# Differential attention in a decoder trunk: the scores of a head as one stretch of row halves in six PSUM banks, the rest of the head in a fixed order behind it

## The chip, the cores and the metric

The kernel runs on one core of one Trainium2 chip. The metric is the device time of one execution, in microseconds (us). Before the change three runs took 1916.96 us in the median (1916.87 to 1918.63).

## The reference

The program is a decoder trunk of two layers over 512 tokens of width 1024, in float32. Each layer is FFN, token mixer, cross-attention, FFN, each closed by a layer norm. The mixer of the first layer is causal differential attention with 8 heads; only this mixer is touched:

```python
def diff_attention(x, w_qkv, w_o, lam_q, lam_k, subln_g, cos, sin, lam_init):
    q, k, v = jnp.split(x @ w_qkv, 3, axis=-1)
    q = rope(q.reshape(B, S, H, 2, dk), c5, s5)      # H = 8, dk = 64: two maps per head
    k = rope(k.reshape(B, S, H, 2, dk), c5, s5)
    v = v.reshape(B, S, H, 2 * dk)
    ...
    def block(args):                                  # blocks of 128 queries
        qblk, i = args
        s = jnp.einsum('bqhcd,bkhcd->bhcqk', qblk, k).astype(jnp.float32) * scale
        s = jnp.where(mask, s, jnp.finfo(jnp.float32).min)
        p = jax.nn.softmax(s, axis=-1)
        a = p[:, :, 0] - lam * p[:, :, 1]
        return jnp.einsum('bhqk,bkhe->bqhe', a.astype(v.dtype), v)
    o = lax.map(block, (qb, jnp.arange(nb)))
    ...
    o = o * lax.rsqrt(jnp.mean(jnp.square(o), axis=-1, keepdims=True) + LN_EPS)
    o = o * subln_g.astype(jnp.float32) * (1.0 - lam_init)
    return o.reshape(B, S, H * 2 * dk).astype(x.dtype) @ w_o
```

## The kernel before

Every float32 operand is split into a high and a low part of a rounded format, and every product is three matmuls (high by high, high by low, low by high; lines L210 to L212 in the projections). Tokens stand in four blocks of 128. A head has 128 rows of q and of k: rows 0 to 63 are its first map, rows 64 to 127 its second.

The mixer is woven from two generators. `da_main` does the projections: v of two heads, then q and k of each head, and after the last of them the output projection of heads 0 to 3. `da_side` does the attention of a head once its q and k are there. `weave` runs the main one, counts its estimated time, and takes one unit of the side whenever enough has passed: `GAP` (900 ns) times the weight that the last unit yielded. The framework's scheduler then fixes one order for each engine, in which high-priority instructions are put early. On the chip each engine works through its own order and waits at its head.

For block i of a head (queries of block i against keys 0 to (i+1)x128) the side does:

- `da_scores`: the scores of both maps on TensorE (PE). For i = 0 and 1 both maps come from one matmul per term into one PSUM bank (L1154), by keys that `da_key` has copied apart into tiles `low` with zeros in the other map's rows (`keys_apart`; four copies per head on ScalarE, L1139). For i = 2 and 3 each map has its own bank, and the matmul uses only its 64 rows of the array (L1159). Then, for each map, one VectorE instruction adds the mask, negates, writes the result to `p` in SBUF and takes the row minimum (L1164, with a read of the accumulator), and ScalarE takes the exponential with its row sum (L1167).
- `da_mix`: on VectorE, the reciprocal of the second map's sum, the coefficient, and p0 + coefficient x p1 (L1176, L1177, L1178).
- `da_turn`: the i+1 blocks of p are transposed on PE (L496, tile `pt`), and split into the pair `a` by ScalarE and VectorE (L125, L126).
- `da_out`: the product with v on PE (L1199, L1200, tile `po`). After blocks 1 and 3 ScalarE copies (L1205), VectorE adds (L1206), ScalarE squares with a sum (L1209). After block 3 GpSimd works out the norm's factor f (L1216 to L1219).
- `da_scale`: o times f on ScalarE (L1228; for the last head half on VectorE); `da_turn_out`: o is transposed on PE (L496) and split.

The side works by steps over all blocks of all heads: in step s it does the scores of block s, the mix of block s-1, the turn of block s-2, the output of block s-3, the scale of a head five steps behind its last block, and the turn of its output six behind.

The banks for `sc`, `pt` and `po` come from three PSUM pools in turn (px, py, yz, two buffers each: six banks); the projections have two further banks.

Of the kernel before, what the change touches and what calls it, by code (L numbers as in the profile page):

```python
# [17 lines left out]
P = 128  # L18
D = 1024
S = 512  # L20
NT = S // P
# [7 lines left out]
DA_H = 8  # L29
# [4 lines left out]
NEG = -float(2.0**100)  # L34
# [1 line left out]


V_FIRST, LEAD, GAP = 6, 6000, 900
W_SC, W_T, W_O, W_E = (1.1, 1.4, 1.8, 2.2), (0.5, 0.7, 0.9, 1.1), (0.4, 0.8, 0.6, 1.1), (0.6, 0.8)
LM, LT, LO, LS = 1, 2, 3, 5  # L40
HALVES = (slice(0, DA_DK), slice(DA_DK, P))

FFN_TURNS = (((0, 1, 2), ()), ((3, 4), (0, 1)), ((5, 6), (2, 3)), ((7, 8), (4, 5)), ((9, 10), (6, 7)))
# [53 lines left out]
WAIT = object()  # L97


def drain(units):  # L100
    for _ in units:
        pass
# [7 lines left out]
class Trunk:  # L110
# [80 lines left out]
    def mm(self, name):  # L191
        return self.mmp.tile([P, S], F32, tag="mm", name=name)
# [937 lines left out]

    def da_key(self, ps):


        k, t = self.pair("qk"), self.da_rope(ps)
        apart = self.keys_apart[len(self.heads) % 2]
        self.split(k[0], k[1], t)
        for whole, part in zip(k, apart):
            for m, rows in enumerate(HALVES):
                self.nc.scalar.copy(part[rows, m], whole[rows, : 2 * P].bitcast(F32))  # L1139
        return k, apart  # L1140

    def da_scores(self, st, i):

        nc = self.nc
        q, k, n = st["q"], st["k"], (i + 1) * P
        qi, kn = slice(i * P, n), slice(0, n)
        mx, rc, cf = self.small("mx"), self.small("rc", (P, 1)), self.small("cf", (P, 1))
        sm = st["sm"][:, i]
        mm, terms = nc.tensor.matmul, ((0, 0), (1, 0), (0, 1))
        if i < 2:  # L1150
            both = self.aux("sc")[:, : 2 * n].rearrange("p (m n) -> p m n", m=2)
            sc = [both[:, m] for m in range(2)]
            for a, b in terms:
                mm(both, q[a][:, qi], k[1][b][:, :, kn], start=a == b, stop=b == 1)  # L1154
        else:
            sc = [self.aux("sc")[:, :n] for m in range(2)]
            for a, b in terms:
                for m, rows in enumerate(HALVES):
                    mm(sc[m], q[a][rows, qi], k[0][b][rows, kn], start=a == b, stop=b == 1)  # L1159
        p = [self.tmp("p")[:, :n] for m in range(2)]  # L1160
        with self.tc.high_priority():
            for m in range(2):
                least = mx[:, m : m + 1]
                nc.vector.tensor_tensor_reduce(  # L1164
                    p[m], sc[m], self.mask[:, S - n :], -1.0, -NEG, ALU.add, ALU.min, least
                )
                nc.scalar.activation(  # L1167
                    p[m], p[m], AF.Exp, bias=least, scale=-1.0, accum_out=sm[:, m : m + 1]
                )
        st["m", i] = p, sm, rc, cf  # L1170

    def da_mix(self, st, i):

# [89 lines left out]

    def da_side(self):

        n = DA_H * NT
        for s in range(n + LS + 2):
            h, i = divmod(s, NT)
            if s < n:
                while h >= len(self.heads) or self.clock < self.heads[h][0] + LEAD:  # L1270
                    yield WAIT
                self.da_scores(self.heads[h][1], i)
                yield W_SC[i]
            h, i = divmod(s - LM, NT)
            if 0 <= s - LM < n:
                self.da_mix(self.heads[h][1], i)
            h, i = divmod(s - LT, NT)
            if 0 <= s - LT < n:
                self.da_turn(self.heads[h][1], i)
                yield W_T[i]  # L1280
            h, i = divmod(s - LO, NT)
            if 0 <= s - LO < n:
                while len(self.heads[h][1]["v"]) < NT:
                    yield WAIT
                self.da_out(self.heads[h][1], i)
                yield W_O[i]
            h, i = divmod(s - LS, NT)
            if 0 <= s - LS < n and i == NT - 1:
                self.da_scale(self.heads[h][1])
                yield W_E[0]  # L1290
            h, i = divmod(s - LS - 1, NT)
            if 0 <= s - LS - 1 < n and i == NT - 1:
                self.oT[h] = self.da_turn_out(self.heads[h][1])
                yield W_E[1]

    def diff_attention(self, layer, ln):
        self.keys_apart = [self.pair("low", (P, 2, 2 * P)) for i in range(2)]
        for pair in self.keys_apart:
            for t in pair:
                for m, rows in enumerate(HALVES):  # L1300
                    self.nc.gpsimd.memset(t[rows, 1 - m].bitcast(F32), 0.0)
# [459 lines left out]
```

## Time and profile before

| what | before |
| --- | --- |
| median of three runs | 1916.96 us |
| the profiled execution | 1915.99 us, its span 1914.2 us |
| PE busy | 1898.0 us (99%) |
| VectorE (DVE) busy | 1551.7 us (81%) |
| ScalarE (ACT) busy | 1016.6 us (53%) |
| GpSimd (POOL) busy | 319.3 us (17%) |
| granted TensorE clock, mean | 0.999 |

The span runs from the first to the last instruction of one profiled execution. PE counts matmuls, PEld the weight loads that overlap them. A row of the timeline has the start in us, the duration in us, engine, line, operation, output and inputs, shapes and count; in square brackets the idle time before it and what ended it. Matmuls are pipelined: a row's duration is longer than the distance to the next one's start, and it is the distance that counts. The same holds for VectorE and ScalarE. The attention lies between 340 and 560 us.

### The profile page before, as it was taken

The page shows a single profiled execution, that of the slowest core. Times are in us where ns is not written, and L with a number is a line of the kernel's source. Part 1 is how long each engine was busy: PE and PEld are TensorE (multiplying, and loading weights), DVE is VectorE, ACT ScalarE, POOL GpSimd, SP SyncE. Part 2 cuts the span into 40 slices and gives each one's busy share as a digit, 9 for nine tenths or more (in the row PEclk, how much of TensorE's full clock was granted, in tenths as well). Part 3 has the DMA queues.
Part 4 walks back from the last instruction along what each step waited for, and adds up shares of the span by engine and source line. Part 5 has one row for each costly group of instructions (what it writes and reads, how often), then busy time and mean ns, then how long its engine had stood idle before and what let it go on. Part 6 is the DMA issues. An engine that isn't in the chain of part 4 may idle for free.

```text
span 1914.2 us, 32507 instructions
## 1 busy us (share of the span) xinstructions
PE 1898.0 (99%) x13088; PEld 1732.0 (90%) x13088; DVE 1551.7 (81%) x2250; ACT 1016.6 (53%) x1578; POOL 319.3 (17%) x282
## 2 busy tenths in 40 slices
PE   9999999999999999999999999999999999999998
PEld 8999998888879888999998999999898889999996
DVE  7888889888867558889888988898787568998886
ACT  6555454566745435655553655555455436555552
POOL 3112121111110002221220311212130012211210
PEclk9999999999999999999999999999999999999999
DMA  9978772332225317987785687878344438867861
GB/s 249 215 176 177 177 139 78 91 89 67 89 67 161 116 60 194 193 175 164 143 191 171 117 180 166 181 164 186 101 132 133 137 84 174 178 156 168 189 130 54
DMA packets 246743, 277.96 MB, mean 145 GB/s; under 512 B 8256, under 2 KB 212544, under 8 KB 246592
## 3 DMA queue, kind: packets, MB, share of 16 engines
q0 software_dynamic: 92928, 92.29, 31.5%
q1 hardware_dynamic: 153664, 183.59, 29.9%
q8 instruction: 103, 1.69, 0.4%
q14 instruction: 48, 0.39, 0.1%
HBM read 273.75 MB, written 2.10 MB: 144 GB/s over the span
## 4 chain that ended last, share of the span: by engine, by line
PE 82%; DVE 11%; ACT 3%; DMA 2%; issue 1%; POOL 1%; SPq 0%; DVEq 0%; ACTq 0%; POOLq 0%
PE x L210 7%; PE x L211 7%; PE x L212 7%; PE z L210 4%; PE z L211 4%; PE z L212 4%; PE ps L210 4%; PE ps L212 4%; PE ps L211 4%; PE px L212 2%; PE px L210 2%; PE px L211 2%; PE y L212 2%; PE y L210 2%; PE y L211 2%; PE pz L212 1%
## 5 line engine op out<-in xcount | busy, mean ns | idle before, releaser
L715 POOL DMA_DIRECT2D ra<-in_ffn_w_in_dram x132 | 170.8, 1316 | 981.8 <-DVE wl L722 966.2
L720 ACT CAST wh<-ra 128x1024 fp32r<-128x1024 f32 x176 | 185.1, 1054 | 206.9 <-PE x L211 65.7
L722 DVE TENSOR_TENSOR wl<-ra,wh 128x1024 fp32r<-128x1024 f32 x176 | 214.2, 1222 | 66.5 <-ACT wh L720 66.1
L210 PE MATMUL x<-xe,wh 128*128 128x256 f32 x704 | 194.8, 277 | 0.0
L211 PE MATMUL x<-xe,wh 128*128 128x256 f32 x704 | 194.6, 276 | 0.0
L212 PE MATMUL x<-xe,wl 128*128 128x256 f32 x704 | 194.5, 276 | 0.0
L720 ACT CAST wh<-rc 128x1024 fp32r<-128x1024 f32 x132 | 138.9, 1053 | 101.6 <-PE x L211 41.4
L125 ACT CAST wh<-b 128x1024 fp32r<-128x1024 f32 x112 | 117.8, 1051 | 130.5 <-PE x L211 67.2
L722 DVE TENSOR_TENSOR wl<-rc,wh 128x1024 fp32r<-128x1024 f32 x132 | 160.0, 1220 | 24.9 <-ACT wh L720 24.9
L126 DVE TENSOR_TENSOR wl<-b,wh 128x1024 fp32r<-128x1024 f32 x112 | 136.8, 1221 | 40.2 <-ACT wh L125 40.2
L210 PE MATMUL x<-xh,wh 128*128 128x256 f32 x536 | 148.5, 277 | 0.0
L211 PE MATMUL x<-xl,wh 128*128 128x256 f32 x536 | 148.2, 276 | 0.0
L212 PE MATMUL x<-xh,wl 128*128 128x256 f32 x536 | 148.2, 276 | 0.0
L211 PEld LDWEIGHTS x<-xe,wh 128*128 128x128 f32 x704 | 132.3, 188 | 1.4
L210 PEld LDWEIGHTS x<-xe,wh 128*128 128x128 f32 x704 | 132.1, 188 | 1.3
L212 PEld LDWEIGHTS x<-xe,wl 128*128 128x128 f32 x704 | 132.2, 188 | 0.0
L126 DVE TENSOR_TENSOR wl<-raw,wh 128x1024 fp32r<-128x1024 f32 x64 | 82.2, 1288 | 42.0 <-ACT wh L125 41.2
L211 PEld LDWEIGHTS x<-xl,wh 128*128 128x128 f32 x536 | 100.7, 188 | 0.7
L210 PEld LDWEIGHTS x<-xh,wh 128*128 128x128 f32 x536 | 100.6, 188 | 0.7
L212 PEld LDWEIGHTS x<-xh,wl 128*128 128x128 f32 x536 | 100.6, 188 | 0.0
L125 ACT CAST wh<-raw 128x1024 fp32r<-128x1024 f32 x64 | 66.4, 1048 | 60.6 <-PE xq L211 20.2
L210 PE MATMUL z<-xe,wh 128*128 128x256 f32 x352 | 97.4, 277 | 0.0
(451 smaller groups left out, 6289.7 us busy)
## 6 DMA issues: line engine op xcount, KB each, us to landing
ra<-in_ffn_w_in_dram POOLq DMA_DIRECT2D x132, 512.0 KB, 6.9
rc<-in_ffn_w_in_dram SPq DMA_DIRECT2D x88, 512.0 KB, 5.9
b<-in_ffn_w_out_dram SPq DMA_DIRECT2D x76, 512.0 KB, 4.8
ra<-in_ffn_w_in_dram SPq DMA_DIRECT2D x44, 512.0 KB, 5.0
rc<-in_ffn_w_in_dram POOLq DMA_DIRECT2D x44, 512.0 KB, 7.5
raw<-in_xa_wkv_dram SPq DMA_DIRECT2D x16, 1024.0 KB, 5.4
raw<-in_da_w_qkv_dram SPq DMA_DIRECT2D x16, 512.0 KB, 5.2
raw<-in_xa_wq_dram SPq DMA_DIRECT2D x8, 1024.0 KB, 5.2
```

The costliest lines, as they stand in the source:

```text
L125: self.nc.scalar.copy(hi, src),
L126: self.nc.vector.tensor_sub(lo, src, hi.bitcast(F32)),
L210: self.first_mm = mm(out, w[0], x[0], start=start, stop=False, skip_group_check=again)
L211: mm(out, w[0], x[1], start=False, stop=False, skip_group_check=again)
L212: self.last_mm = mm(out, w[1], x[0], start=False, stop=stop, skip_group_check=again)
L715: nc.gpsimd.dma_start(t, source(*block), accum_op=ALU.add)
L720: hi = nc.scalar.copy(v[0], raw)
L722: lo = nc.vector.tensor_sub(v[1], raw, v[0].bitcast(F32))
```

## The change

The copies apart (`keys_apart`, their zeroing on GpSimd and the four ScalarE copies per head) go. `da_scores` now does a whole head: all matmuls of its four blocks stand in one stretch, each on the 64 rows of its map, 24 of them (4 blocks x 3 terms x 2 maps), in the block order 1, 0, 2, 3. They take six banks at once: two for block 1, two that blocks 2 and 0 share, two for block 3. Behind it come the mask, minimum and exponential of all blocks in the same order. `da_side` goes head by head: scores, the turn of the previous head's output, then the fixed list `STEPS`, then the scale. The pool `p` has 8 buffers instead of 6.

```diff
-W_SC, W_T, W_O, W_E = (1.1, 1.4, 1.8, 2.2), (0.5, 0.7, 0.9, 1.1), (0.4, 0.8, 0.6, 1.1), (0.6, 0.8)
-LM, LT, LO, LS = 1, 2, 3, 5
+W = dict(scores=2.0, turn=(1.0, 1.0, 1.2, 1.5), out=(0.6, 0.8, 1.2, 2.0), scale=0.8, last=0.8)
+STEPS = (
+    ("mix", 1), ("mix", 0), ("mix", 2), ("turn", 0), ("mix", 3), ("turn", 1),
+    ("out", 0), ("turn", 2), ("out", 1), ("turn", 3), ("out", 2), ("out", 3),
+)
+SC_ORDER = (1, 0, 2, 3)
...
     def da_key(self, ps):
-        k, t = self.pair("qk"), self.da_rope(ps)
-        apart = self.keys_apart[len(self.heads) % 2]
-        self.split(k[0], k[1], t)
-        for whole, part in zip(k, apart):
-            for m, rows in enumerate(HALVES):
-                self.nc.scalar.copy(part[rows, m], whole[rows, : 2 * P].bitcast(F32))
-        return k, apart
+        k = self.pair("qk")
+        self.split(k[0], k[1], self.da_rope(ps))
+        return k
...
+    def da_scores(self, st):
+        one, two, three = ([self.aux("sc") for m in range(2)] for i in range(3))
+        banks = {
+            0: [t[:, 3 * P :] for t in two],
+            1: [t[:, : 2 * P] for t in one],
+            2: [t[:, : 3 * P] for t in two],
+            3: three,
+        }
+        for i in SC_ORDER:
+            qi, kn = slice(i * P, (i + 1) * P), slice(0, (i + 1) * P)
             for a, b in terms:
                 for m, rows in enumerate(HALVES):
+                    mm(banks[i][m], q[a][rows, qi], k[b][rows, kn], start=a == b, stop=b == 1)
+        for i in SC_ORDER:
...
     def da_side(self):
+        for h in range(DA_H):
+            while h >= len(self.heads) or self.clock < self.heads[h][0] + LEAD:
+                yield WAIT
+            st = self.heads[h][1]
+            self.da_scores(st)
+            yield W["scores"]
+            if h:
+                self.oT[h - 1] = self.da_turn_out(self.heads[h - 1][1])
+                yield W["last"]
+            for step, i in STEPS:
+                if step == "out":
+                    while len(st["v"]) < NT:
+                        yield WAIT
+                getattr(self, "da_" + step)(st, i)
+                if step != "mix":
+                    yield W[step][i]
+            self.da_scale(st)
+            yield W["scale"]
...
-            bufs = dict(low=4, rt=2, a=4, p=6, o=2, qk=8, _x=0, v=4, oT=11, mask=1)
+            bufs = dict(low=4, rt=2, a=4, p=8, o=2, qk=8, _x=0, v=4, oT=11, mask=1)
```

Lines of the changed program stand ten or fewer behind those of the old one (L1162 is the score matmul, L1171 the mask and minimum, L1174 the exponential, L1183 to L1185 the mix, L1235 the scale, L1212 the copy of o, L1216 the squares). How it moves instructions is shown at three places of head 1; rows are the engine's order, with line, operation, output and inputs, shape, and a count where equal ones follow each other.

PE at the scores of head 1 (`v` and `q` are projections). Before, one block's scores between two steps of the projection of v:

```order
L212 MATMUL v<-wh,xl 128x256
L1154 MATMUL sc<-low,qk 128x512 x3
L210 MATMUL v<-wh,xh 128x256
L211 MATMUL v<-wl,xh 128x256
L212 MATMUL v<-wh,xl 128x256
```

Now:

```order
L222 MATMUL v<-wh,xl 128x256
L1162 MATMUL sc<-qk 128x256 x6
L1162 MATMUL sc<-qk 128x128 x6
L1162 MATMUL sc<-qk 128x384 x6
L1162 MATMUL sc<-qk 128x512 x6
L220 MATMUL v<-wh,xh 128x256
```

All four blocks now stand together. Behind them PE has 18 matmuls of v, four transposes of the previous head's o, 6 matmuls of v, and then the transpose of p of block 0, which needs the mix of block 0.

VectorE at the mix of block 0 of head 1 (`p` tiles are numbered; `mx` rows read the minimum; `rc` and `cf` are reciprocal and coefficient). Before, that mix follows its own block's minimum:

```order
L1164 ISA p_4332,mx_4325<-sc_4328,mask_3828 128x128
L1164 ISA mx_4325 128x1
L1164 ISA p_4333,mx_4325<-sc_4328,mask_3828 128x128
L1164 ISA mx_4325 128x1
L1176 RECIPROCAL rc_4326<-sd_4205 128x1
L1177 SCALAR_TENSOR_TENSOR cf_4327<-sd_4205,nlam_4033,rc_4326 128x1
L1178 SCALAR_TENSOR_TENSOR p_4332<-p_4333,cf_4327,p_4332 128x128
```

Now (p_4415 is block 0; the rows of 128x384 and 128x512 are blocks 2 and 3):

```order
L1171 ISA p_4425,mx_4421<-sc_4376,mask_3816 128x384
L1171 ISA mx_4421 128x1
L1171 ISA p_4433,mx_4430<-sc_4377,mask_3816 128x512
L1171 ISA mx_4430 128x1
L1171 ISA p_4434,mx_4430<-sc_4378,mask_3816 128x512
L1171 ISA mx_4430 128x1
L1183 RECIPROCAL rc_4413<-sd_4235 128x1
L1183 RECIPROCAL rc_4422<-sd_4235 128x1
L1184 SCALAR_TENSOR_TENSOR cf_4414<-sd_4235,nlam_4021,rc_4413 128x1
L1184 SCALAR_TENSOR_TENSOR cf_4423<-sd_4235,nlam_4021,rc_4422 128x1
L1185 SCALAR_TENSOR_TENSOR p_4415<-p_4416,cf_4414,p_4415 128x128
```

The mix of block 0 now stands behind the minima of all four blocks; in heads 1, 3, 5, 6 and 7 the reciprocal, coefficient and mix of block 1 stand between the minima of block 1 and those of block 0.

ScalarE at the exponentials of head 1. Before, the scale of head 0 has one block's exponentials behind it:

```order
L1209 ACTIVATE po,sq<-o 128x128
L1228 ACTIVATE o<-o,f 128x128 x3
L1167 ACTIVATE p,sd<-p,mx 128x512 x2
L125 CAST a<-pt 128x256
L130 ACTIVATE qk<-rt 128x512
```

Now:

```order
L1212 COPY o<-po 128x256
L135 CAST v<-v 128x4x128
L1216 ACTIVATE po,sq<-o 128x128 x2
L1235 ACTIVATE o<-o,f 128x128 x4
L1174 ACTIVATE p,sd<-p,mx 128x256 x2
L1174 ACTIVATE p,sd<-p,mx 128x128 x2
L1174 ACTIVATE p,sd<-p,mx 128x384 x2
L1174 ACTIVATE p,sd<-p,mx 128x512 x2
```

All exponentials of head 1 stand behind the four scales of head 0, and those behind the last squares of head 0; so it is in heads 3, 5, 6 and 7 too, while in heads 2 and 4 the scales stand far ahead.

More of the change, by code (lines that the diff above doesn't have):

```diff
@@ L38 @@
 V_FIRST, LEAD, GAP = 6, 6000, 900
-W_SC, W_T, W_O, W_E = (1.1, 1.4, 1.8, 2.2), (0.5, 0.7, 0.9, 1.1), (0.4, 0.8, 0.6, 1.1), (0.6, 0.8)
-LM, LT, LO, LS = 1, 2, 3, 5
+W = dict(
+    scores=2.0,
+    turn=(1.0, 1.0, 1.2, 1.5),
+    out=(0.6, 0.8, 1.2, 2.0),
+    scale=0.8,
+    last=0.8,
+)
+STEPS = (
+    ("mix", 1), ("mix", 0), ("mix", 2), ("turn", 0), ("mix", 3), ("turn", 1),
+    ("out", 0), ("turn", 2), ("out", 1), ("turn", 3), ("out", 2), ("out", 3),
+)
+SC_ORDER = (1, 0, 2, 3)
 HALVES = (slice(0, DA_DK), slice(DA_DK, P))
@@ L1131, in da_key @@
     def da_key(self, ps):
-        k, t = self.pair("qk"), self.da_rope(ps)
-        apart = self.keys_apart[len(self.heads) % 2]
-        self.split(k[0], k[1], t)
-        for whole, part in zip(k, apart):
-            for m, rows in enumerate(HALVES):
-                self.nc.scalar.copy(part[rows, m], whole[rows, : 2 * P].bitcast(F32))
-        return k, apart
-    def da_scores(self, st, i):
-        nc = self.nc
[L1145 to L1156, printed above, removed]
+        k = self.pair("qk")
@@ new lines, in da_key @@
+        self.split(k[0], k[1], self.da_rope(ps))
+        return k
+    def da_scores(self, st):
+        nc = self.nc
+        q, k, mm, terms = st["q"], st["k"], self.nc.tensor.matmul, ((0, 0), (1, 0), (0, 1))
+        one, two, three = ([self.aux("sc") for m in range(2)] for i in range(3))
[7 more added lines that the diff above has]
+            qi, kn = slice(i * P, (i + 1) * P), slice(0, (i + 1) * P)
@@ L1157, in da_scores @@
             for a, b in terms:
                 for m, rows in enumerate(HALVES):
[L1159 to L1169, printed above, removed]
@@ L1170, in da_scores @@
-        st["m", i] = p, sm, rc, cf
+                    mm(banks[i][m], q[a][rows, qi], k[b][rows, kn], start=a == b, stop=b == 1)
+        for i in SC_ORDER:
+            n = (i + 1) * P
+            mx, rc, cf = self.small("mx"), self.small("rc", (P, 1)), self.small("cf", (P, 1))
+            sm = st["sm"][:, i]
+            p = [self.tmp("p")[:, :n] for m in range(2)]
+            with self.tc.high_priority():
+                for m in range(2):
+                    least = mx[:, m : m + 1]
+                    nc.vector.tensor_tensor_reduce(
+                        p[m], banks[i][m], self.mask[:, S - n :], -1.0, -NEG, ALU.add, ALU.min, least
+                    )
+                    nc.scalar.activation(
+                        p[m], p[m], AF.Exp, bias=least, scale=-1.0, accum_out=sm[:, m : m + 1]
+                    )
+            st["m", i] = p, sm, rc, cf
@@ L1264, in da_side @@
     def da_side(self):
[L1266 to L1294, printed above, removed]
@@ L1296, in diff_attention @@
-    def diff_attention(self, layer, ln):
[L1297 to L1301, printed above, removed]
+        for h in range(DA_H):
[16 more added lines that the diff above has]
+            yield W["scale"]
@@ L1302, in diff_attention @@
+        self.oT[h] = self.da_turn_out(st)
+        yield W["last"]
+    def diff_attention(self, layer, ln):
         self.mask = self.act("mask", (P, S), mybir.dt.bfloat16)
```

## Prediction

> **What bounds the kernel now.** I read the page first (busy shares, the chain that ended last), then the attention stage by windows, then the timelines of PE, VectorE and ScalarE in it.
>
> ```profile
> span 1914.2 us, 32507 instructions
> PE 82%; DVE 11%; ACT 3%; DMA 2%; issue 1%; POOL 1%; SPq 0%; DVEq 0%; ACTq 0%; POOLq 0%
> 340.00:560.00 220.00, 218.51 (x1300) 182.32 (x1299) 175.35 (x441) 137.46 (x373) 37.84 (x51) 1.00 0.28 85
> ```
>
> The last row is the stage: of 220 us PE is idle for 1.5, VectorE for 45, ScalarE for 83. PE sets the end here, so the change is worth what it takes from PE's own work, less every wait that it puts into PE's order.
>
> **What it takes from PE.** The distance between starts is the price of a matmul.
>
> ```profile
> 368.95 0.51 PE L1154 MATMUL sc<-low,qk 128*128 128x256 f32 x3
> 369.30 0.40 PE L210 MATMUL k<-xh,wh 128*128 128x512 f32 x1
> ...
> 370.00 0.85 PE L1154 MATMUL sc<-low,qk 128*128 128x512 f32 x3
> 370.69 0.40 PE L210 MATMUL k<-xh,wh 128*128 128x512 f32 x1
> ...
> 371.86 0.40 PE L212 MATMUL k<-xh,wl 128*128 128x512 f32 x1
> 372.19 0.79 PE L1159 MATMUL sc<-qk 64*128 64x384 f32 x6
> ...
> 373.25 0.40 PE L211 MATMUL k<-xl,wh 128*128 128x512 f32 x1
> ...
> 379.83 0.22 PE L1200 MATMUL po<-v,a 128*128 128x128 f32 x1
> 379.89 0.33 PE L210 MATMUL v<-wh,xh 128*128 128x256 f32 x1
> ```
>
> Three matmuls of 256 columns take 0.35 (369.30-368.95), of 512 columns 0.70, so 0.117 and 0.232 each; 128 columns take 0.06. The stretch of six row halves with 384 columns takes 373.25-371.86, less the two paces of 0.232 that stand there anyway: 0.93. Six matmuls one behind the other would take 6x0.174 (three quarters of 0.232) = 1.04, and more with any cost of switching; three pairs side by side take 0.52. So the halves run side by side, and entering and leaving the row-half mode costs 0.40. By that a stretch of six with 512 columns takes 3x0.232 + 0.40 = 1.10.
>
> A head before: 0.35 + 0.70 + 0.93 + 1.10 = 3.08. Now one stretch: 3x(0.06+0.117+0.174+0.232) + 0.40 = 2.15. That is 0.93 less per head, 7.4 for eight. The pairs with 128 columns are the one new form; if they only kept the pace of 256 columns, each head would lose 3x0.057, 1.4 in all. In head 7 the new order splits the last six matmuls by three of the output projection: one more switch, 0.40, and one pair taken apart, 0.23. **Gain 6.7 us.** The four copies per head off ScalarE and the zeroing off GpSimd are worth nothing here: neither engine is the bound.
>
> **What it puts into PE's order.** Before, the turn of a block came a whole step after its mix. Now the transpose of block 0 stands, in head 1, 24 matmuls of 256 columns and four transposes behind the scores.
>
> ```profile
> 389.90 0.60 PE L496 MATMUL pt<-ident,p 128*128 128x128 f32 x4
> 390.25 0.48 PE L210 MATMUL q<-xh,wh 128*128 128x512 f32 x1
> 390.57 0.39 PE L211 MATMUL q<-xl,wh 128*128 128x512 f32 x1
> ```
>
> Four transposes cost 0.67-0.23 = 0.44. Let T be the start of the first score pair; of the 0.40 for switching, 0.10 lies before it. PE is at that transpose at T + 1.75 + 0.30 + 24x0.117 + 0.44 = T+5.3. VectorE must by then have done, in the order shown, the minima of all four blocks and two mixes:
>
> ```profile
> 384.03 0.29 DVE L1164 CUSTOM_DVE_ANT_0 p<-sc,mask 128x128 f32<-128x128 f32 x1
> 384.25 0.08 DVE L1164 DVE_READ_ACCUMULATOR2_ANT mx<- 128x1 f32 x1
> ...
> 388.34 0.42 DVE L1164 CUSTOM_DVE_ANT_0 p<-sc,mask 128x256 f32<-128x256 f32 x1 [0.63 <-PE sc L1154]
> 388.69 0.08 DVE L1164 DVE_READ_ACCUMULATOR2_ANT mx<- 128x1 f32 x1
> ...
> 393.34 0.56 DVE L1164 CUSTOM_DVE_ANT_0 p<-sc,mask 128x384 f32<-128x384 f32 x1
> 393.82 0.08 DVE L1164 DVE_READ_ACCUMULATOR2_ANT mx<- 128x1 f32 x1
> ...
> 395.28 0.16 DVE L1176 RECIPROCAL rc<-sd 128x1 f32<-128x1 f32 x1 [0.90 <-ACT p L1167]
> 395.48 0.22 DVE L1177 SCALAR_TENSOR_TENSOR cf<-sd,nlam,rc 128x1 f32<-128x1 f32 x1
> 395.73 0.62 DVE L1178 SCALAR_TENSOR_TENSOR p<-p,cf 128x384 f32<-128x384 f32 x1
> ...
> 399.29 0.68 DVE L1164 CUSTOM_DVE_ANT_0 p<-sc,mask 128x512 f32<-128x512 f32 x1
> 399.90 0.08 DVE L1164 DVE_READ_ACCUMULATOR2_ANT mx<- 128x1 f32 x1
> ```
>
> One minimum of 128, 256, 384, 512 columns takes 0.22, 0.35, 0.48, 0.61; the next one starts with the read. Two maps of four blocks: 3.3. Reciprocal and coefficient take 0.2 and 0.25 when each waits for the one before. From the scores to the minimum:
>
> ```profile
> 387.44 0.86 PE L1154 MATMUL sc<-low,qk 128*128 128x512 f32 x3
> ```
>
> The third of these starts 0.46 on, at 387.90; the minimum starts at 388.34, 0.44 later, and with 256 columns 0.12 earlier. Block 1 is then ready at T + 0.10 + 2x0.117 + 0.32 = T+0.65.
>
> ScalarE comes between, since the mix of block 1 needs its exponentials and, in heads 1, 3, 5, 6 and 7, stands ahead of the other minima:
>
> ```profile
> 388.98 0.49 ACT L1167 ACTIVATE p<-p,mx 128x256 f32<-128x256 f32 x1
> ...
> 389.47 0.49 ACT L1167 ACTIVATE p<-p,mx 128x256 f32<-128x256 f32 x1
> ...
> 394.55 0.60 ACT L1167 ACTIVATE p<-p,mx 128x384 f32<-128x384 f32 x1
> ```
>
> One exponential of 256 columns takes 0.49; from the start of the second to the reciprocal is 395.28-394.55 = 0.73 for 384 columns, some 0.62 for 256.
>
> ```profile
> 427.59 0.41 DVE L1206 TENSOR_TENSOR o<-o,po 128x256 f32<-128x256 f32 x1
> ...
> 428.47 0.28 ACT L1209 ACTIVATE po<-o 128x128 f32<-128x128 f32 x1
> ...
> 430.31 0.99 ACT L1228 ACTIVATE o<-o,f 128x128 f32<-128x128 f32 x3 [1.44 <-POOL f L1219]
> 431.21 0.71 ACT L1167 ACTIVATE p<-p,mx 128x512 f32<-128x512 f32 x1
> ```
>
> These show ScalarE waiting for GpSimd's f (second square to scale 1.84) with an exponential behind three scales (0.30 each). Now all exponentials of heads 1, 3, 5, 6, 7 stand behind four. From the last output matmul: 0.6 for the copy (an estimate: 0.2 as from scores to minimum less the matmul's own pace, and 0.4 as of a pass of this width), add to scale 430.31-427.59 = 2.7, four scales 1.2: ScalarE is free 4.5 us behind it. PE has only 24 matmuls of 256 columns (2.8) and 0.1 there, so that is T+1.6, against T+1.1 when the minimum is ready.
>
> Head 1 by steps: exponentials of block 1 at T+1.6 and 2.1, reciprocal 2.7, coefficient 2.9, mix 3.2 to 3.55, then 2.6 of minima (0.43+0.96+1.22) to 6.2, two reciprocals and coefficients 0.7, mix of block 0 with its way to PE 0.4: T+7.3. **PE waits 2.0**, where it waited for nothing. Behind it the mixes of blocks 2 and 3 and a weight split stand before the low part of block 0, and output 0 waits 0.3 more. Head 3 has the same order: 2.3 each.
>
> Heads 2 and 4: no scales in the way, but the next head's q ended only 1.4 (six matmuls of 512 columns) before the scores, and its rotation stands first on VectorE:
>
> ```profile
> 398.07 0.74 DVE L1119 STREAM_SHUFFLE rt<-q 128x512 f32<-128x512 f32 x1
> ...
> 398.89 1.30 POOL L1121 TENSOR_TENSOR rt<-rt,ropeS 128x512 f32<-128x512 f32 x1 [17.63 <-DVE rt L1119]
> ...
> 400.51 0.69 DVE L1122 TENSOR_TENSOR rt<-rt 128x512 f32<-128x512 f32 x1
> ```
>
> Shuffle to GpSimd 0.8, GpSimd 1.3, the sum 0.65: with 0.2 ahead of it VectorE is free 2.95 after q's end, which is T+1.45, 0.8 late. Then 3.3 of minima, 0.6 and 0.6 for q's low part and a weight split, 0.8 for reciprocals and coefficients, two mixes 0.8: T+7.6 against T+5.3, 2.3 each. Head 0 has one split more and only 12 matmuls of 512 columns (2.8) between scores and transpose, but more time ahead: T+7.4 against T+4.9, 2.5.
>
> Head 5 has q's rotation ahead of the add, the squares and so of f: the scales end at T+2.9 instead of T+1.6, and it waits 1.3 more than head 1, 3.3. In head 6 they end at T+3.0, 1.4 more; k's rotation stands between the last minimum and the mix of block 0 and adds 2.4 (0.8 + 1.3 + 0.6 less what else runs in it, 0.3); PE comes 0.7 later: 2.0 + 1.4 + 2.4 - 0.7 = 5.1. Head 7 has the split stretch and more of the output projection ahead, PE at T+6.4 against T+7.3: 0.9. Sum: 2.5 + 2.3 + 2.3 + 2.3 + 2.3 + 3.3 + 5.1 + 0.9 = 21.0, **21 us**.
>
> Bounds of the waits: with VectorE free at T+0.65 and ScalarE at once, the chain ends at T+6.8, 1.5 in a typical head and 11 in all; if each head went like head 6, 41. I take 21, built from the orders themselves, nearer to the low end since nothing in the trace makes every head like head 6. Waits that PE has today in the stage (1.5) I leave as they are.
>
> [...]
>
> **Sum.** 1914.2 - 6.7 + 21 = 1928.5 of span; with the 1.8 between span and time (1915.99-1914.2), 1930.3. The profiled execution lies 1.0 under the median, so 1931.
>
> **Rivals.** (a) *The saving decides; faster.* PE's waits for the mix stay under 0.35 on average, so under 3 of the 6.7. For it: VectorE's 45 idle us in the stage. Against it: idle in the stage does not help a queue that must do four blocks of minima in order. About 1911. (b) *The short end.* VectorE and ScalarE are ready in time, VectorE finding the coefficient of block 1 early too, waits of 7 to 10: 1917 to 1920, no change by what can be told apart here (0.2%, 3.8 us). (c) *Banks.* The scores take all six banks, the sixth last held by the squares of the previous head, which end some 2 us after its last output; the sixth is wanted 4 after it. If the squares queue behind casts by 3 instead of 0, five heads wait 1 more each: 1936. (d) *The clock.* Waits of 3 to 5 us are new; in the whole stage PE idled 1.5.
>
> ```profile
> 1.25 3.17 PE L120 MATMUL idle<-hb 128*128 128x512 bf16 x7 [1.25 <-DVE hb L569]
> 4.21 2.01 PE L496 MATMUL pt<-ident,X 128*128 128x128 f32 x8
> ```
>
> After the idle start seven matmuls of 512 columns took 2.96, 0.42 each instead of 0.23. If each head's wait brings this back for as many, 8x7x0.19 = 11 us more: 1942. [...]
>
> **How the numbers follow.** Forecast 0.57, its own range 1923 to 1940; (a) 0.10; (b) 0.16; (c) 0.12; (d) 0.05. The range 1918 to 1941 leaves out (a), the lower edge of (b) and the far end of (d). Faster 0.10; same 0.16; slower 0.74.
>
> **What would show it.** Right: score pairs start together and a stretch costs 2.1 to 2.2; PE's waits list the transpose of p behind the mix of VectorE, eight times, 1 to 5 us, longest in head 6; ScalarE's exponentials start behind the scales. Wrong: those waits sum to less than 7; or PE waits before the scores rather than behind them (c); or the pairs do not overlap at 128 columns; or the granted clock falls in the stage (d).

## The result, and the profile after

| what | before | after |
| --- | --- | --- |
| median (runs) | 1917.09 us (1916.87 to 1918.63, 4) | 1940.37 us (1939.35 to 1943.91, 4) |
| the profiled execution | 1915.99 us, span 1914.2 us | 1939.43 us, span 1937.6 us |
| PE busy | 1898.0 us (99%) | 1901.4 us (98%) |
| granted TensorE clock, mean | 0.999 | 0.995 |

The ratio is 1.0124, 95% interval 1.0111 to 1.0136: 23.3 us slower, where 14 were forecast. The median lies inside the stated range (1918 to 1941) by only 0.6 us. First the page's own rows of the changed kernel (the span; the chain that ended last, by engine) and the window of the attention stage. Such a window row has the stretch, its length, the busy time of PE, PEld, VectorE, ScalarE and GpSimd, each with its number of instructions, then the granted clock, the DMA share and GB/s.

```profile
span 1937.6 us, 32560 instructions
PE 80%; DVE 12%; ACT 3%; DMA 2%; issue 2%; POOL 1%; SPq 0%; DVEq 0%; POOLq 0%; ACTq 0%
340.00:560.00 220.00, 200.17 (x1236) 170.25 (x1235) 163.91 (x418) 119.34 (x321) 36.57 (x49) 0.96 0.23 70
```

PE is still the engine that sets the end, but in these 220 us it is now idle for 20 instead of 1.5, it gets fewer instructions through (1236 against 1300), and its clock, 1.00 before, is 0.96. All of the difference lies in this stage: from 6 us before the first score matmul to the first matmul of the next stage (the memory's keys) before needed 216.2 us, after 239.3, and 23.1 is the growth of the whole span (23.4) but for 0.3.

I made an account of PE over that stretch by the distances between the starts of its matmuls. Each distance is its matmul's own pace (0.232 for 512 columns, 0.117 for 256 and so on), and what is over is put down to a half clock if it lies in such a window, to a wait if it is over 0.25, and to switching and small losses otherwise. The numbers are worked out, not rows of a view; records missing from a trace move something between the first two columns, so they are read together, and a column is good to some 0.5 us.

| us | stage | paces | switching, small losses | waits | half clock |
| --- | --- | --- | --- | --- | --- |
| before | 216.2 | 195.4 | 18.8 | 1.9 | 0 |
| after | 239.3 | 192.2 | 16.4 | 22.8 | 7.5 |

The work itself fell by 5.6 (214.2 to 208.6), waits rose by 20.9, and 7.5 came from the clock. The list of PE's waits in the changed kernel (weight loads, which meet the wait first: 20.0 at the transposes against 17.6 on the matmuls; total, times, longest) says where:

```profile
PEld pt L506 <- DVE p L1185: 20.0, 7, 5.0
PEld sc L1162 <- DVE mx L1171: 2.6, 1, 2.6
```

Seven waits are transposes of block 0 behind VectorE's mix, in heads 0 to 6. The eighth, in head 7, is inside the scores: its last three matmuls, which belong to block 3, wait until VectorE has done a minimum of block 2. VectorE comes to that minimum late, because it waits for ScalarE's exponentials of block 1 first:

```profile
552.51 0.16 DVE L1183 RECIPROCAL rc<-sd 128x1 f32<-128x1 f32 x1 [1.84 <-ACT p L1174]
```

```profile
554.40 0.96 PE L1162 MATMUL sc<-qk 64*128 64x512 f32 x3 [2.14 <-DVE mx L1171]
```

I take what matmul and minimum share to be a bank of PSUM; which bank ties these two was not traced. On PE's timeline head 1 looks like this:

```profile
388.19 0.28 PE L222 MATMUL v<-wh,xl 128*128 128x256 f32 x1
388.40 2.18 PE L1162 MATMUL sc<-qk 64*128 64x256 f32 x24
390.51 0.39 PE L220 MATMUL v<-wh,xh 128*128 128x256 f32 x1
390.74 0.28 PE L221 MATMUL v<-wl,xh 128*128 128x256 f32 x1
...
393.77 0.28 PE L222 MATMUL v<-wh,xl 128*128 128x256 f32 x1
395.47 0.33 PE L506 MATMUL pt<-ident,p 128*128 128x128 f32 x1 [1.42 <-DVE p L1185]
```

Measured as the prediction measured a stretch, up to the second matmul behind it, the score stretch takes 390.74 - 388.19 - 2x0.117 = 2.32, where 2.15 was worked out. So the saving is 0.76 a head and not 0.93. Most of the difference lies in the pairs of 128 columns: the two matmuls of a pair start within 0.004 of each other, but two of three pairs keep a distance of 0.11 to the next pair instead of 0.06. PE is at the transpose at T+5.5 (T = 388.40) and gets it at T+7.1. In between, ScalarE's first exponential and VectorE's end of the minima in the same head:

```profile
390.04 0.50 ACT L1174 ACTIVATE p<-p,mx 128x256 f32<-128x256 f32 x1
```

```profile
394.00 0.69 DVE L1171 CUSTOM_DVE_ANT_0 p<-sc,mask 128x512 f32<-128x512 f32 x1
394.61 0.09 DVE L1171 DVE_READ_ACCUMULATOR2_ANT mx<- 128x1 f32 x1
394.61 0.22 DVE L1183 RECIPROCAL rc<-sd 128x1 f32<-128x1 f32 x2
```

They come at T+1.6 and T+6.2. ScalarE and VectorE in head 6, the longest wait:

```profile
516.48 1.28 ACT L1235 ACTIVATE o<-o,f 128x128 f32<-128x128 f32 x4 [1.42 <-POOL f L1226]
517.67 0.50 ACT L1174 ACTIVATE p<-p,mx 128x256 f32<-128x256 f32 x1
```

```profile
521.63 0.69 DVE L1171 CUSTOM_DVE_ANT_0 p<-sc,mask 128x512 f32<-128x512 f32 x1
...
522.25 0.73 DVE L1129 STREAM_SHUFFLE rt<-k 128x512 f32<-128x512 f32 x1
...
524.60 0.69 DVE L1132 TENSOR_TENSOR rt<-rt 128x512 f32<-128x512 f32 x1 [0.93 <-POOL rt L1131]
525.21 0.34 DVE L1184 SCALAR_TENSOR_TENSOR cf<-sd,nlam,rc 128x1 f32<-128x1 f32 x2
525.47 0.87 DVE L1185 SCALAR_TENSOR_TENSOR p<-p,cf 128x128 f32<-128x128 f32 x2
```

The exponentials (L1174) stand behind the four scales (L1235); after the last minimum the rotation of k (L1129 to L1132, by way of GpSimd) stands ahead of the mix (L1185), and PE's transpose starts at 525.87, 11.6 behind the scores at 514.27.

The clock is seen by cutting windows where it changes. Three pairs of the changed kernel, each 3.41 us and the 3.41 us behind it:

```profile
422.23:425.64 3.41, 1.27 (x8) 0.76 (x6) 3.41 (x18) 3.41 (x13) 0.56 (x2) 1.00 0.00 0
425.64:429.06 3.42, 3.41 (x10) 2.72 (x11) 2.51 (x8) 1.50 (x4) 0.07 (x1) 0.50 0.00 0
473.43:476.85 3.42, 1.62 (x9) 0.97 (x8) 3.42 (x19) 3.18 (x11) 0.31 (x1) 1.00 0.62 199
476.85:480.26 3.41, 3.06 (x18) 2.61 (x19) 3.41 (x12) 2.46 (x6) 0.32 (x2) 1.00 0.29 111
497.33:500.74 3.41, 1.31 (x7) 1.10 (x8) 3.34 (x15) 3.41 (x10) 0.71 (x2) 1.00 0.00 0
500.74:504.15 3.41, 3.41 (x12) 2.91 (x11) 3.41 (x8) 1.04 (x4) 1.28 (x1) 0.50 0.00 0
```

At 425.64 and at 500.74 the granted clock (third number from the end) is 0.50 for just such a stretch: PE is busy all the time, with 10 and 12 matmuls. There are five such stretches in the stage (524.63 to 531.46 is two, 555.35 the fifth), none before, and they cost 7.5, 1.5 each. The first two pairs stand at waits of the same length, 2.32 (heads 2 and 4), and only the first of them halves the clock; what tells them apart comes out of the runs with idle time by itself.

### The profile page after: what moved, and what is told of

It is laid out like the page before. It is cut to its first block, busy times and chain, and to the rows that moved or that the text cites. A ratio compares the mean times of both kernels' runs of the same rounds, so it can differ in the third digit from the quotient of the medians.

```text
span 1937.6 us, 32560 instructions
## 1 busy us (share of the span) xinstructions
PE 1901.4 (98%) x13136; PEld 1737.7 (90%) x13136; DVE 1552.2 (80%) x2250; ACT 1005.7 (52%) x1546; POOL 317.1 (16%) x274
## 4 chain that ended last, share of the span: by engine, by line
PE 80%; DVE 12%; ACT 3%; DMA 2%; issue 2%; POOL 1%; SPq 0%; DVEq 0%; POOLq 0%; ACTq 0%
PE x L220 7%; PE x L221 7%; PE x L222 7%; PE z L220 4%; PE z L221 4%; PE z L222 4%; PE ps L220 4%; PE ps L222 4%; PE ps L221 4%; PE px L220 2%; PE px L222 2%; PE px L221 2%; PE y L222 2%; PE x L757 2%; PE y L221 2%; PE y L220 2%
## 5 line engine op out<-in xcount | busy, mean ns | idle before, releaser
L136 DVE TENSOR_TENSOR wl<-b,wh 128x1024 fp32r<-128x1024 f32 x112 | 137.0, 1223 | 40.4 <-ACT wh L135 39.9
L136 DVE TENSOR_TENSOR wl<-raw,wh 128x1024 fp32r<-128x1024 f32 x64 | 85.0, 1332 | 45.2 <-ACT wh L135 44.5
```

The costliest lines, as they stand in the source:

```text
L136: self.nc.vector.tensor_sub(lo, src, hi.bitcast(F32)),
```

## The experiments

Each run stands beside runs of the kernel before on the same chip (1916.24 us for the first four, 1916.38 for the next two, 1915.91 for the last three). The question: what costs the time, the closeness of the rest of the head to its scores, VectorE's queue, the six banks, or the clock?

**More of PE's work behind the scores.** The weight of the scores is tripled, so the weave puts more projection matmuls between the scores and the first step.

```diff
-    scores=2.0,
+    scores=6.0,
```

> The changed kernel with one number changed: the weight behind the scores is 6.0 instead of 2.0, so PE has about 3.6 us more of projections between the score stretch and the transpose of p of block 0. Theory (waits and clock): the extra 23 us are 22.6 us of PE waiting for the mix (20.0) and inside the scores of head 7 (2.6), and some 8.5 us from five windows of 3.4 us at half the granted clock, less 6.7 us gained on the scores. Then with PE at that transpose at T+8.8 or later against mixes ready at T+7.3 to T+8.6, the waits for the mix sum to under 4 us, the clock stays at 1.00, and the time is 1910 to 1915, under that of before. Rival (the stretch itself is dear, six banks at once): removing the wait for the mix moves the wait to the banks; the time stays over 1925.

Measured: 1939.66 us (1937.67 to 1940.64), ratio 1.0119 (1.0104 to 1.0134). Nothing was won. Its list of PE's waits:

```profile
PEld po L1207 <- DVE a L136: 12.6, 7, 4.4
PEld po L1206 <- ACT a L135: 3.8, 4, 1.9
PEld sc L1162 <- DVE mx L1171: 2.3, 1, 2.3
PEld pt L506 <- DVE p L1185: 2.2, 2, 1.7
```

The wait at the transpose is all but gone (2.2 are left) and stands one step later, at output 0 (`po`), for the low part of `a` (L136). In head 1 VectorE does that low part behind the mixes of blocks 2 and 3, the rotation of q and a split of weights (1.97 us), while between transpose and output 0 PE has only 1.6 to 2.3 us of work by its paces. So the wait belongs to the whole chain scores, minima, exponentials, mix, transpose, split, output, not to one place in it.

**Filling the waits.** Dummy matmuls of 384 columns into a part of the transposes' bank that is overwritten after, as many per head as the wait holds, so that PE is late by the same but not idle.

```diff
+FILL = (17, 8, 13, 8, 13, 19, 33, 0)
...
+        if i == 0:
+            q = st["q"][0]
+            for _ in range(FILL[st["h"]]):
+                self.nc.tensor.matmul(pt[:, : 3 * P], q[:, :P], q[:, P:], start=True, stop=True)
```

> The changed kernel with matmuls without use (384 columns, into the bank that the transpose of p of block 0 then overwrites) put ahead of that transpose, as many as fill the wait of each head: 17, 8, 13, 8, 13, 19, 33 and none in head 7, 0.174 us each. PE still cannot go on sooner, but it does not idle. Theory (clock): the granted clock stays at 1.00 in the stage and the time falls by the clock's share, about 8.5 us, to 1930 to 1934. Rival (the windows at half clock lie in the waits or beside work that hides them, and the waits are all): 1938 to 1942, as the changed kernel.

Measured: 1942.79 us (1941.31 to 1943.2), ratio 1.0135 (1.0118 to 1.0152). As a test of the clock it miscarried: the dummies moved the scheduler's order on VectorE, and new waits came at output 0.

```profile
PEld po L1213 <- DVE a L137: 5.9, 4, 3.1
PEld pt L507 <- DVE p L1186: 3.0, 7, 1.0
PEld sc L1163 <- DVE mx L1172: 2.6, 1, 2.6
```

Waits fell from 22.8 to 10.3 and half-clock stretches from five to two, while the dummies took 111 x 0.174 = 19. It agrees with a clock that answers to idle time, but doesn't show it.

**Minima of blocks 2 and 3 behind the mix of block 0.** This takes the four longest minima from ahead of the mix in VectorE's queue; the mixes of blocks 2 and 3 come later for it.

```diff
+    ("mix", 1), ("mix", 0), ("least", 2), ("least", 3), ("mix", 2), ("turn", 0), ("mix", 3), ("turn", 1),
...
+        for i in SC_ORDER[:2]:
+            self.da_least(st, i)
...
+            behind = self.tc.issue_after(st["mixed"].ins) if i > 1 else nullcontext()
```

> The changed kernel with one order changed on VectorE: the minima of blocks 2 and 3 are issued behind the mix of block 0 instead of ahead of it. Theory (the queue of VectorE): 2.2 us less stand ahead of the mix of block 0 in every head, so the waits of PE there fall from 20.0 us to 5 to 8, some 3 us come back at the turn of block 2, the clock stays up in most heads, and the time is 1917 to 1925. Rival (the exponentials on ScalarE behind the scales set the mix, not VectorE's minima): the waits fall by under 6 us, and the time stays over 1930.

Measured: 1932.7 us (1929.51 to 1935.02), ratio 1.0082 (1.0067 to 1.0097). The time is the rival's (over 1930); the waits lie between the two.

```profile
PEld pt L506 <- DVE p L1193: 11.7, 9, 2.5
PEld po L1214 <- ACT a L135: 5.3, 5, 1.5
PEld sc L1162 <- DVE mx L1179: 2.7, 1, 2.7
```

In the profiled run, the slowest of the four, the transposes wait 8 less and the half clock costs 3.1 instead of 7.5 (two stretches); outputs wait 5.3 that they didn't. So VectorE's queue of minima makes some 8 of the 20. In what is left VectorE itself waits for ScalarE: in head 5 it is idle for 1.80 before the reciprocal of block 1 and for 0.73 before that of block 0, with the exponentials behind the four scales. The rest moved to the outputs.

**Row halves alone.** The kernel before, with blocks 0 and 1 by row halves too, each block a stretch of its own at its old step, no keys apart.

```diff
-            both = self.aux("sc")[:, : 2 * n].rearrange("p (m n) -> p m n", m=2)
...
+        sc = [self.aux("sc")[:, :n] for m in range(2)]
+        for a, b in terms:
+            for m, rows in enumerate(HALVES):
+                mm(sc[m], q[a][rows, qi], k[b][rows, kn], start=a == b, stop=b == 1)
```

> The kernel before with one part of the change alone: the scores of blocks 0 and 1 by row halves too, and no keys copied apart; the order of the side is that of before, so each block's scores are a stretch of their own with its own switching. Theory (0.40 us per stretch for switching, pairs side by side at 128 and 256 columns too): a head pays 0.58 and 0.75 instead of 0.35 and 0.70, 0.28 more, 2.2 us in all: 1918.5 to 1920.5. If the pairs at 128 columns do not run faster than those at 256: 1.4 more, 1920 to 1922. Rival (the copies apart on ScalarE hold something up): not slower than before, 1917 or less.

Measured: 1919.45 us (1917.83 to 1921.47), ratio 1.0014 (1.0004 to 1.0023): 3.2 more, where 2.2 to 4.3 stood for the first theory. No gain from the copies taken off ScalarE is seen. The stretches of 256, 384 and 512 columns cost 0.75, 0.92 and 1.09, which is three paces and 0.39 to 0.40 for the change into the row-half mode and back. That of 128 columns costs more than the 0.58 of the theory:

```profile
383.37 0.28 PE L212 MATMUL v<-wh,xl 128*128 128x256 f32 x1
383.58 0.55 PE L1149 MATMUL sc<-qk 64*128 64x128 f32 x6
...
384.28 0.28 PE L211 MATMUL v<-wl,xh 128*128 128x256 f32 x1
```

384.28 - 383.37 - 2x0.117 = 0.68, so here too the pairs of 128 columns don't run at half the pace of 256. In the list of waits the changes of mode stand as time in which PE waits for nothing that the profile shows (4.0 in 11 places before):

```profile
PEld sc L1149 <- issue: 7.3, 20, 0.4
```

So the change saves PE's work only by joining stretches; the halves by themselves lose.

**The saving with the steps of before.** Three kernels keep the order of before, with its distance of a step or more between scores, mix, turn and output, and join stretches: all four blocks in one, with output four steps behind; two stretches of two blocks; and blocks 2 and 3 alone.

```diff
+STRETCH, LEAST = {0: (0, 1, 2, 3)}, ((1, 0), (2,), (3,), ())
-LM, LT, LO, LS = 1, 2, 3, 5
+LM, LT, LO, LS = 1, 2, 4, 6
...
+        if i in STRETCH:
+            self.da_stretch(st, STRETCH[i])
+        for j in LEAST[i]:
+            self.da_least(st, j)
```

> One stretch per head of all four blocks in six banks, as in the change, but the rest of the head in the steps of before: minima of blocks 1 and 0, then 2, then 3, in the steps that follow; mix one step behind, turn two behind, output four behind (ahead of the turn of its step), scale six behind; 8 buffers of p. Theory (PE waits only because the chain from scores to turn and output has too little of PE's work beside it): the whole 7.4 is kept, waits at the turns gone: 1907 to 1913 against 1916.2. Rival (six banks at once are the cost: they are held by the previous head's turns and outputs, or, while the minima go through, keep the next ones from starting): waits of 8 or more before scores, turns or outputs, 1918 or more; with half-clock windows behind them 1922 or more.

```diff
+STRETCH, LEAST = {0: (0, 1), 2: (2, 3)}, ((1, 0), (), (2,), (3,))
```

> The order of before in all but the scores: two stretches of row halves per head, blocks 0 and 1 (in one pair of banks) at the step where block 0 stood, blocks 2 and 3 at the step of block 2; the minima of blocks 1, 0 follow the first, of block 2 and then, a step later, of block 3 the second; no keys apart, 8 buffers of p. Theory (the saving on PE is real, and what costs is only that the rest of the head stands too close behind the scores): a head costs 3x(0.06+0.117) + 0.40 and 3x(0.174+0.232) + 0.40 on PE = 2.55 instead of 3.08, 4.2 less in eight heads; the waits in the stage stay under 2.5 in sum and the granted clock at 1.00: 1910 to 1914 against 1916.2 on this chip. Rival (any such stretch makes PE wait for banks or for the mix, wherever the rest stands): waits of 5 or more in the stage, 1917 or more.

```diff
+        elif i == 2:
+            for j in (2, 3):
+                n = (j + 1) * P
+                st["sc", j] = [self.aux("sc")[:, :n] for m in range(2)]
...
+        if i > 1:
+            sc = st.pop(("sc", i))
```

> The kernel before with a single edit: the matmuls of block 3 stand directly behind those of block 2, in one stretch of row halves; blocks 0 and 1 by the keys apart as before, minima and all else in the steps of before. Theory (entering and leaving the row-half mode costs 0.40 each time, and this takes away one of two such costs a head without waits): 3.2 less, 1912 to 1915 against about 1916.4. Rival (the banks of block 3 are wanted a step sooner, while turns and outputs of the head before still hold them): waits inside the stretch, 0.2 to 0.4 a head, which eat it: 1915.5 to 1918.

| kernel | median us | ratio to before (95%) | stage | paces and small losses | waits | half clock |
| --- | --- | --- | --- | --- | --- | --- |
| before | 1916.38; 1915.91 | | 216.2 | 214.2 | 1.9 | 0 |
| one stretch, far | 1918.50 | 1.0010 (1.0001 to 1.0019) | 218.6 | 208.5 | 9.9 | 0 |
| two stretches | 1917.35 | 1.0004 (0.9995 to 1.0013) | 217.5 | 212.6 | 4.7 | 0 |
| blocks 2 and 3 | 1914.49 | 0.9994 (0.9985 to 1.0002) | 215.7 | 211.1 | 4.4 | 0 |

The first has the change's 24 matmuls in six banks, with the blocks in the order 0 to 3 and blocks 0 and 1 in one pair of banks: PE's work falls by 5.7, as in the change (5.6), but the wait for a mix is down to one of 0.9, and the clock stays at 1.00. What is left of the waits is another kind. In its list for the stage:

```profile
PEld po L1207 <- DVE mx L1172: 4.1, 3, 1.7
PEld sc L1153 <- ACT po L1217: 1.8, 1, 1.8
PEld sc L1153 <- DVE a L127: 1.4, 1, 1.4
PEld pt L497 <- DVE p L1186: 0.9, 1, 0.9
```

The releasers of the first three are what last used a bank: a minimum (L1172), the squares (L1217), the low part of a transpose (L127). So the 20 us at the turns and the half clock come from closeness and not from the banks: that much of the theory held. The time and the 8.0 of added waits are the rival's: with the chain out of the way, most of what is left is the price of six banks at once (7.3 in the first three rows), and it is more than the gain. The minima come a step apart here and so hold the banks longer than in the change; how much of the 7.3 that makes, no run separates.

Two stretches won 1.6 of PE's work by the account, not 4.2, and lost it again by 2.8 of waits. Half of the missing 2.6 is in the first stretch, which costs 1.09 instead of 0.93 in every head, its pairs of 128 columns again; the second costs the 1.62 that was worked out where it doesn't wait, and the other half of the 2.6 was not traced. As for the waits, in three heads the second stretch took 0.1 to 1.1 longer from first to last start; I take busy banks for the cause (the list of waits has scores behind the low part of a transpose twice, 1.2 in all). Joining blocks 2 and 3 alone took off 3.1 of work, near the 3.2 expected (1.62 a head instead of 0.92 and 1.09), and gave 2.5 back in waits, most of it at one output (1.3) and one transpose (0.9). The median is 1.4 lower, and its interval holds 1. It is the fastest of the kernels run, but it can't be told from before.

**Idle time by itself.** The kernel before, with PE made idle once a head at the turn of block 0: PE transposes a spare tile, GpSimd raises a column of it to a power (twice, or four times), and PE transposes it again. The order on PE is that of before, with two to five matmuls between the two.

```diff
+        if i == 0:
+            nc, z = self.nc, self.z
+            nc.tensor.transpose(pt[:, 3], z, self.ident)
+            for _ in range(2):
+                nc.gpsimd.tensor_tensor(z[:, :1], z[:, :1], self.mhalf[:, :1], ALU.pow)
+            nc.tensor.transpose(pt[:, 2], z, self.ident)
```

> The kernel before, with an idle time made on PE alone, once a head, at the turn of block 0: one more transpose of a spare tile, two power operations of one column on GpSimd on that tile, and a second transpose that waits for them (the spare columns of that bank are not read by anything else). By the rows of the page a power takes 1.0 to 1.1 us, so with some 0.3 of signals and less the 0.2 to 0.5 of PE's work that stands between the two transposes PE idles 2.0 to 2.3, eight times, 17 in all; PE's order is otherwise that of before, and VectorE's nearly so. Theory (waits of this length, whatever causes them, sometimes bring half-clock windows, as in the change): one to five windows of about 3.4 us with a granted clock of a half, each costing 1.5, so 1935 to 1941. Rival (the clock fell in the change for another reason, and idle times of 2 us do not touch it): granted clock 1.00 through the stage and 1931 to 1935.

> As the run with the short idle time, but four power operations, so that PE idles 3.7 to 4.0 at each of the eight places, 31 in all. Theory: more half-clock windows than with the short idle times, about one for each place, 8 x 1.5 = 12: 1955 to 1962. Rival (the clock does not answer to idle times): 1.00 throughout, 1945 to 1950.

Measured: 1927.94 us (1926.57 to 1930.03), ratio 1.0065 (1.0049 to 1.008), with two; 1943.42 us (1941.07 to 1946.71), ratio 1.0143 (1.0129 to 1.0157), with four. A power took 0.56 us here and not the 1.0 to 1.1 that I had read from other rows, so both idle times are about two thirds of what was meant (11.7 instead of 17 in all, 21.2 instead of 31), and it is the long run that tests 2 us. One row of the list of waits from each:

```profile
PEld pt L1189 <- POOL idle L1188: 11.7, 8, 2.2
```

```profile
PEld pt L1189 <- POOL idle L1188: 21.2, 8, 3.9
```

With the short one (no gap between matmuls over 1.9) the stage is 11.5 longer, which is the waits (9.9 more) and 16 transposes, and the clock is 1.00: no window. With the long one the stage is 29.5 longer, of which 19.9 are waits and 9.5 half clock, in six stretches. The two runs differ only in two more powers on GpSimd at each place, so here it was the longer idle time on PE (3.9 instead of 2.2 at the longest) that brought the half clock. Windows of the long run:

```profile
374.52:377.93 3.41, 1.42 (x13) 1.21 (x11) 2.60 (x9) 1.89 (x5) 2.59 (x5) 1.00 0.00 0
377.93:381.35 3.42, 3.42 (x16) 2.46 (x15) 2.46 (x7) 2.02 (x6) 0.88 (x1) 0.50 0.03 7
398.41:401.83 3.42, 1.61 (x10) 1.23 (x8) 1.00 (x3) 0.75 (x4) 1.97 (x3) 1.00 0.23 57
401.83:405.24 3.41, 2.61 (x16) 2.02 (x18) 0.98 (x4) 1.50 (x5) 0.67 (x2) 1.00 0.00 0
487.16:490.58 3.42, 2.07 (x12) 1.60 (x10) 2.69 (x8) 2.24 (x5) 1.52 (x3) 1.00 0.00 0
490.58:493.99 3.41, 2.58 (x16) 2.00 (x18) 1.64 (x5) 0.93 (x4) 1.95 (x3) 1.00 0.00 0
```

The windows are laid on a grid of 3.41 us through the places where the clock changed. A gap (what the distance between two starts has over the matmul's pace) of 2.16 that ends at 377.61 lies in one window, PE is busy 1.42 of it, and the next is halved. A longer gap, 2.77, ends at 402.63: it is split over two windows, PE is busy 1.61 and 2.61, and neither is followed by a half clock. One of 2.34 is split at 490.58 in the same way.

## Why the prediction was right or wrong

**PE's work: right in kind, two terms mis-sized.** 6.7 less was forecast, 5.6 is found in the account. The pairs do start side by side (within 0.01 in head 1), and joining saves the 0.40 per stretch (0.39 where blocks 2 and 3 were joined alone). But the stretch costs 2.32 instead of 2.15: the 0.17 is as much as the prediction gave for pairs of 128 columns at the pace of 256, "1.4 in all", and then left out of the sum. In head 7 all three pairs of the last six matmuls are taken apart, which is 3x0.232 = 0.70 and not 0.23. The copies off ScalarE brought nothing that the row halves alone could show.

**The waits at the turn of block 0: right in place and cause for heads 0 to 6; that the sum fits is luck.** Forecast by heads: 2.5, 2.3, 2.3, 2.3, 2.3, 3.3, 5.1, 0.9; measured as gaps: 2.62, 1.58, 2.32, 1.57, 2.32, 3.43, 4.97, and 2.31 in head 7; 21.1 against 21.0. So there were seven such waits, not eight. The chain of head 1 was foreseen to 0.1 us up to the last minimum (exponentials at T+1.6, VectorE's minima done at T+6.2), and its end 0.2 too late. Two terms were off by 1.4 each, against each other, and so the sum came out to 0.1 by chance: heads 1 and 3 wait 0.7 less each, the 0.3 at their output 0 among it, which didn't come; in head 7 it was not the mix but the scores themselves that waited, for a minimum that stood behind ScalarE, 1.4 more. PE waiting for a bank, if it was one, is the kind of rival (c), in a head for which it was not foreseen. Rival (c) in its own place, five heads waiting for the squares' bank, didn't come in the change; in the kernel with one stretch far ahead it did, once (1.8).

**The clock: the step that failed.** The sum held no term for it, and rival (d) had a chance of 0.05, because I weighed waits one by one and by their length: "waits of 3 to 5 us are new". That the length of a wait decides was not shown. The half clock came in four places, two of them behind waits of 2.3, and cost 7.5; of the signs of being wrong that the prediction names, this one ("the granted clock falls in the stage") came. With 1.1 for the smaller gain, less 0.1 for the waits, that is what lies between the 14.3 forecast and the 22.8 of the account. The measured 1940.37 lies past the forecast's own range (1923 to 1940): the stated range held because its upper edge had been set towards (d), to which the sum gave no weight. The price in (d), 11 for eight heads or 1.3 each, was near; five stretches came, at 1.5 each. The run with the long idle time shows the half clock without the change (six stretches, 9.5).

The changes of the clock in the changed kernel lie on a grid whose step is the length of a single halved stretch, 3.413: 425.64 to 500.74 is 22 windows of 3.413, 500.74 to 524.63 seven, 531.46 to 555.35 seven. And a gap of 2.2 us sufficed where it fell in one window (2.16, in the long run with idle time).

**What the change was worth otherwise.** (a) and (b) are excluded by the waits. The experiments say why the saving can't be had for nothing: with the rest of the head close behind, the chain is waited for; with it far behind, the banks are.

## What to carry to other kernels

When several small steps are joined into one stretch on the bound engine, walk the whole chain that hangs on it, in the order in which each other engine will do it: what PE saves by the stretch (0.76 a head, 5.6 in all by the account) was lost more than three times over (20.9) to a chain that before ran beside a step of other work. Cover put in at one place only showed the next wait. And idle time on PE cost twice where it fell in one window of the grid: the wait itself (2.16 in one place of the long run with idle time, 2.32 in head 2 of the change), and a stretch at half clock behind it (7.5 for five in the change, 9.5 for six in the long run). Price the narrowest form of a new stretch from a run of its own, since here it did not scale from the wider ones (mostly 0.11 a pair at 128 columns instead of 0.06).

## What the runs showed of the hardware

In these runs the half clock follows a grid, not the length of a gap. In the five profiles in which it occurs (the change, more work behind the scores, the filled waits, the later minima, the long idle time), I cut the stage by the grid and read PE's busy time in every window of full clock. All 15 windows with 1.43 us or less were followed by a clock of 0.50; of those with 1.61 or more none; of the two between, 1.50 was not and 1.59 was. So whether a half clock followed a wait of some 2 us depended on where the wait fell: 2.16 in one window was followed by it, 2.77 and 2.34 split over two were not (the long idle time). Runs of the same kernel differ in the clock: of the later minima, the run of 1929.51 has a mean clock of 0.999 and that of 1935.02 one of 0.997; that the place of the waits makes this was not shown. Of the 16 halved windows that began a stretch, 12 stayed alone, and PE was busy through all of these. Four were followed by a second one, as in 524.63 to 531.46 in the change; in three of these four PE was busy for 1.62 to 2.18 of the first, in the fourth for all of it, so what ends the half clock stays open.

Entering and leaving the row-half mode cost 0.39 to 0.41 a stretch, seen in three ways: in the stretch before (0.93 for 384 columns against 0.52), in the row halves alone (0.75, 0.92 and 1.09 for stretches of six with 256, 384 and 512 columns, against 0.35, 0.52 and 0.70 for three paces), and in the joining of blocks 2 and 3 (1.62 instead of 0.92 and 1.09). Pairs of 64 rows ran side by side at 128 columns too, but mostly at 0.11 a pair (0.060, 0.111 and 0.112 in head 1 of the change), near the 0.117 of 256 columns, and not at 0.06. A power of one column on GpSimd mostly took 0.55 to 0.57 us in the two idle-time runs (medians 0.562 and 0.551), and up to 1.06.
